# Order of the first chunks in a hybrid pool and RG-LRU layer: block 9 weights ahead of token tiles, root diagonals one chunk early, chunk 1 normalised ahead of chunk 0's evacuation

## The chip, the core and the metric

One core of one Trainium2 chip runs the whole layer in one launch. The metric is the device time of that launch in microseconds (us), as a median over several runs. The engines are named as in the profile: PE (matmul) and PEld (its weight load), DVE (VectorE), ACT (ScalarE), POOL (GpSimd), SP (SyncE, which issues all DMAs here).

## The reference, cut to what matters

A layer of one prompt (2048 tokens) and eight short samples (8 tokens each), so 2112 tokens of width 1024:

```python
xn = rms_norm(x, norm_pre)                  # one factor 1/rms per token, one gain per channel
z  = xn @ w_in                              # 1024 -> 4096: pool values, pool gate, lru input, lru gate
y_pool = pool_mixer(z[0:1024])              # windows of 2/4/8/16 tokens, then a 256x256 map per group
y_lru  = rg_lru(causal_conv(z[2048:3072]))  # gates, then a scan over the tokens
mixed  = concat(y_pool * silu(z[1024:2048]), y_lru * silu(z[3072:4096]))
out    = x + rms_norm(mixed @ w_out, norm_post)
```

## The kernel before, in words

Tokens lie along the free dimension in five chunks of 426 (the last has 408); `xn[c]` holds a chunk's normalised inputs in 8 slices `k` of 128 channels. Every product is made from a high and a low part of both operands (`hi = round(x)`, `lo = x - hi`), so a slice costs three matmuls of 426 columns, and one block of 128 output channels of one chunk (`z_k` over `k`, lines 287 to 293) costs 24. Blocks 0 and 1 are the values ("v"), blocks 8 and 9 the gates ("g") of pool group 0.

The 1/rms factors are per token and so lie along columns. They come from a second copy of x with tokens on partitions, in 17 tiles of 128 tokens (`load_tok`, 512 KB each, three slots of three tiles). ACT squares and sums a tile (`tok_square`, line 224); `tok_rsqrt` (lines 226 to 234) makes the factors of a range of tiles with four small DVE and two small ACT instructions; `r_rows(c)` (lines 236 to 246) makes a chunk's row of factors on all partitions: ACT scales pieces of the identity by the factors (line 243, tile `dg`), and PE multiplies an all-ones matrix by each piece (line 245, tile `r` in PSUM). `normalise(c)` (lines 248 to 275) then scales the raw chunk on DVE (line 261), ACT rounds it to the high part (line 269), and DVE or POOL subtracts for the low part (line 278). It can take squares of later tiles along on ACT. Two tiles of `x` are therefore needed before a chunk can start: its transposed copy (`xt`) and the token tiles that it covers.

Chunk 0 is different: its slices are multiplied by the channel gain only (`x_g`, `x_hi`, `x_lo`, lines 592 to 600), the matmuls start at once, and the factors are applied when the four results are read out of PSUM (`pool_evac`, line 323, and line 705, with `r0`, a copy in SBUF of the row of chunk 0). Later, at chunk 2, `normalise(0, r0)` scales chunk 0 for the other blocks.

Everything from line 607 to line 789 is in a `manual_schedule`: each engine runs its instructions in the order in which the lines issue them, and each engine's queue waits in that order. SP's queue holds the loads, in the order of the lines 608 to 630: weights and chunk 0 interleaved, then block 8, token tiles 0 to 3, half of chunk 1, tiles 4 and 5, the other half, tile 6, block 9 (`w9r`), the first pool map, chunk 2. PE's queue: v of chunk 0, block 8 (line 684), block 9 (line 692) with the rows of chunks 0 and 1 after its third slice (`R01_AT`), then v of chunk 1, `r_rows(2)`, gate block 8 of chunk 1, the pool map of chunk 0 (`pool_mm`, tile `y`), gate block 9, and then chunks 2, 3 and 4 (lines 714 to 789), where `r_rows(c + 1)` stands after the last slice of the first value block.

PSUM has two rings of four banks: `z_psum` and `s_psum`.

Of the kernel before, what the change touches and what calls it, by code (L numbers as in the profile page):

```python
# [16 lines left out]
P = 128  # L17
# [44 lines left out]
def hymba_kernel(  # L62
# [19 lines left out]
    nc = tc.nc  # L82
# [152 lines left out]

    def r_rows(c):
        lo, hi = XR[c]
        dg = tp_tile(f"dg{c}")
        R = s_psum(f"r{c}")[:, :hi - lo]
        for i in range(lo // P, (hi - 1) // P + 1):  # L240
            n = min(P, T_ALL - i * P)
            a, b = max(lo, i * P), min(hi, i * P + n)
            nc.scalar.activation(out=dg[:n, a - lo:b - lo], in_=ident[:n, a - i * P:b - i * P], func=AF.Copy,
                                 scale=tok[:n, 2, i:i + 1])
            nc.tensor.matmul(R[:, a - lo:b - lo], lhsT=ones[:n, :], rhs=dg[:n, a - lo:b - lo], start=True, stop=True)
        return R
# [360 lines left out]
    with tc.manual_schedule():  # L607
        stage_w(0, 0, 1)
        load_x(0, 0, 1)
        nc.sync.dma_start(out=parT, in_=par)  # L610
        load_x(0, 1, 2)
        stage_w(1, 0, 1)
        load_x(0, 2, 4)
# [5 lines left out]
        for i in range(4):  # L619
            load_tok(i, slots[i // 3])  # L620
        load_x(1, 0, 4)
        for i in range(4, 6):
            load_tok(i, slots[1])
        load_x(1, 4, 8)
        load_tok(6, slots[2])
        for h in range(2):
            nc.sync.dma_start(out=w9r[h], in_=w_in[9, :, 512 * h:512 * (h + 1)])
        pw0r = raw_tile("pw0r")
        nc.sync.dma_start(out=pw0r, in_=pool_w[0])
        load_x(2, 0, 8)  # L630
        w_hi(0, 0, A)
        w_lo(0, 0, V)
        x_g(0)
        x_hi(0)
        x_g(1)
        x_hi(1)
        x_lo(0, V)
# [25 lines left out]
        w_hi(8, 0, A)  # L663
        w_lo(8, 0, G)
        for i in range(3):
            tok_square(i)
        w_hi(8, 1, A)
        w_lo(8, 1, G)
# [5 lines left out]
        lag = 3  # L674
# [10 lines left out]
        for h in range(2):  # L685
            w_hi(9, h, A)
            w_lo(9, h, G)
        for k in range(KT):
            if k == R01_AT:
                R0, r1 = r_rows(0), r_rows(1)  # L690
                A.copy(out=r0, in_=R0)
            z_k(Z0[3], wt[9], 0, k)
        Es, sgs0 = [], []
# [3 lines left out]
        normalise(1, r1, [V], {3: (7,), 5: (8,), 7: (9,)})  # L697
# [16 lines left out]
        for c in range(1, NCH):  # L714
            n = c + 1 if c < LAST else None
            W = CHUNKS[c][1] - CHUNKS[c][0]
            Z = [z_psum(f"v{j}_{c}")[:, :W] for j in range(2)]
# [16 lines left out]
            if c == 1:  # L734
# [3 lines left out]
                tok_rsqrt(7, 10)  # L738
# [21 lines left out]
            if c == 1:  # L760
# [3 lines left out]
                tok_rsqrt(10, 17)  # L764
                silus()
# [708 lines left out]
```

## Time and profile before

| what | value |
|---|---|
| median of 3 runs | 1203.39 us (1202.67 to 1204.98) |
| profiled execution, its own time | 1200.54 us |
| span of that execution (first to last instruction) | 1198.7 us |
| PE busy | 1169.1 us, 98% of the span |
| DVE, ACT, POOL busy | 829.1, 552.3, 356.5 us |
| mean granted TensorE clock | 0.991 of full speed |

The profiled execution is 2.85 us under the median; 1.84 us of it lie outside the span. All positions below are us from the span's start. A bracket at the end of a timeline row is the idle time of the engine before it and what ended that.

### The profile page before, as it was taken

To read this page: it belongs to the slowest core of one execution; us is meant where nothing else is said; L and a number is where in the kernel's file an instruction comes from. 1 tells how busy PE (TensorE), PEld (TensorE's weight loads), DVE (VectorE), ACT (ScalarE), POOL (GpSimd) and SP (SyncE) were. 2 spreads that over 40 slices of the span, in tenths; PEclk is the share of its full clock that TensorE was granted. 3 is DMA by queue.
4 is the path that set the end of the run, shared out by engine and by line. 5 is a ranking of instruction groups with operands and counts; after the bars stand their busy time and mean duration, and the time that the engine had idled before them with its cause. 6 is when DMAs were issued, how large, how long until landed. Compare 5 with 4: busy or idle time off the path is not lost.

```text
span 1198.7 us, 16264 instructions
## 1 busy us (share of the span) xinstructions
PE 1169.1 (98%) x5794; PEld 1079.4 (90%) x5794; DVE 829.1 (69%) x1201; ACT 552.3 (46%) x1015; POOL 356.5 (30%) x486
## 2 busy tenths in 40 slices
PE   6898999999999999999999999999999999999997
PEld 5798999999999999999999999999978878888886
DVE  4666453435445546888888888889877668887787
ACT  5663221221231125767767676776755243335232
POOL 3224430531251232344333433344310002221332
PEclk9799999999999999999999999999999999999999
DMA  9612353533541110111111111113479767767553
GB/s 338 238 42 73 110 190 117 175 101 118 162 129 52 44 42 33 53 49 44 44 41 45 35 50 49 44 40 105 138 202 296 219 185 205 217 198 232 150 170 129
DMA packets 127905, 146.94 MB, mean 123 GB/s; under 512 B 12432, under 2 KB 87440, under 8 KB 127824
## 3 DMA queue, kind: packets, MB, share of 16 engines
q1 hardware_dynamic: 127824, 145.91, 39.1%
q8 instruction: 45, 0.74, 0.3%
q14 instruction: 36, 0.29, 0.1%
HBM read 106.37 MB, written 39.24 MB: 121 GB/s over the span
## 4 chain that ended last, share of the span: by engine, by line
PE 77%; DVE 8%; DMA 6%; ACT 3%; issue 2%; POOL 1%; SPq 0%; DVEq 0%; ACTq 0%; POOLq 0%
PE p L964 6%; PE p L963 6%; PE p L962 6%; PE u L291 5%; PE u L293 5%; PE u L292 5%; PE lg L291 5%; PE lg L292 4%; PE lg L293 4%; PE v L291 4%; PE v L293 4%; PE v L292 4%; PE g L291 4%; PE g L293 4%; PE g L292 4%; DMA a<-mixed 3%
## 5 line engine op out<-in xcount | busy, mean ns | idle before, releaser
L493 DVE SCALAR_TENSOR_TENSOR xs<-u,parT,xs 128x426 f32<-128x426 f32 (+1 forms) x120 | 109.4, 911 | 46.1 <-ACT xs L489 30.5
L291 PE MATMUL v<-xh,w 128*128 128x426 f32 (+2 forms) x320 | 116.7, 365 | 7.9 <-ACT xh L596 7.5
L291 PE MATMUL g<-xh,w 128*128 128x426 f32 (+1 forms) x320 | 115.4, 361 | 3.1 <-ACT w L584 3.1
L292 PE MATMUL v<-xl,w 128*128 128x426 f32 (+2 forms) x320 | 116.0, 363 | 1.3 <-DVE xl L600 0.7
L955 POOL TENSOR_TENSOR xr<-ac,xr 128x512 f32<-128x512 f32 x28 | 47.6, 1717 | 228.6 <-DVE ac L1093 130.7
L293 PE MATMUL g<-xh,w 128*128 128x426 f32 (+1 forms) x320 | 114.8, 359 | 0.3 <-POOL w L587 0.3
L292 PE MATMUL g<-xl,w 128*128 128x426 f32 (+1 forms) x320 | 114.5, 358 | 0.0
L291 PE MATMUL lg<-xh,w 128*128 128x426 f32 (+1 forms) x320 | 113.7, 355 | 0.0
L293 PE MATMUL v<-xh,w 128*128 128x426 f32 (+2 forms) x320 | 113.7, 360 | 0.0
L291 PE MATMUL u<-xh,w 128*128 128x426 f32 (+1 forms) x320 | 113.7, 355 | 0.0
L292 PE MATMUL lg<-xl,w 128*128 128x426 f32 (+1 forms) x320 | 113.4, 354 | 0.0
L293 PE MATMUL lg<-xh,w 128*128 128x426 f32 (+1 forms) x320 | 113.2, 354 | 0.0
L293 PE MATMUL u<-xh,w 128*128 128x426 f32 (+1 forms) x320 | 113.1, 353 | 0.0
L292 PE MATMUL u<-xl,w 128*128 128x426 f32 (+1 forms) x320 | 113.0, 353 | 0.0
L1255 DVE RECIPROCAL rv<-rv 128x426 f32<-128x426 f32 (+1 forms) x40 | 112.4, 2811 | 0.0
L962 PE MATMUL p<-ws,s 128*128 128x512 f32 (+1 forms) x264 | 102.4, 388 | 0.0
L963 PE MATMUL p<-ws,s 128*128 128x512 f32 (+1 forms) x264 | 102.0, 386 | 0.2 <-DVE ws L109 0.2
L964 PE MATMUL p<-ws,s 128*128 128x512 f32 (+1 forms) x264 | 102.1, 387 | 0.1
L962 PE MATMUL p<-ws,a 128*128 128x512 f32 x192 | 75.7, 394 | 1.0 <-ACT ws L106 1.0
L964 PE MATMUL p<-ws,a 128*128 128x512 f32 x192 | 75.8, 395 | 0.8 <-DVE a L109 0.8
L963 PE MATMUL p<-ws,a 128*128 128x512 f32 x192 | 75.7, 394 | 0.4 <-DVE ws L109 0.4
L354 DVE TENSOR_TENSOR s<-e 128x440 f32<-128x440 f32 (+3 forms) x40 | 29.2, 730 | 66.9 <-ACT e L325 48.2
(225 smaller groups left out, 2810.8 us busy)
## 6 DMA issues: line engine op xcount, KB each, us to landing
a<-mixed SPq DMA_DIRECT2D x112, 256.0 KB, 4.2
wr<-in_w_in SPq DMA_DIRECT2D x56, 256.0 KB, 3.1
tok<-in_x SPq DMA_DIRECT2D x16, 512.0 KB, 11.1
wo<-in_w_out SPq DMA_DIRECT2D x32, 256.0 KB, 3.6
wtd<-wo SPq DMA_DIRECT2D x32, 256.0 KB, 2.4
w<-wtd SPq DMA_DIRECT2D x32, 256.0 KB, 3.7
xr<-in_x SPq DMA_DIRECT2D x32, 256.0 KB, 3.7
out<-xr SPq DMA_DIRECT2D x30, 256.0 KB, 2.6
```

What stands on the lines that cost most here:

```text
L291: nc.tensor.matmul(out, lhsT=wh, rhs=xh, start=(k == 0), stop=False)
L292: nc.tensor.matmul(out, lhsT=wh, rhs=xl, start=False, stop=False)
L293: nc.tensor.matmul(out, lhsT=wl, rhs=xh, start=False, stop=(k == KT - 1))
L354: nc.vector.tensor_tensor(out=dst[:, first:L], in0=src[:, first:L], in1=src[:, first - sh:L - sh], op=ALU.add)
L493: nc.vector.scalar_tensor_tensor(out=xs, in0=E[:, k:k + n], scalar=col(C_CW + 8 * k, b), in1=xs, op0=ALU.mult, op1=ALU.add)
L955: (eng or nc.vector).tensor_tensor(out=out, in0=a, in1=b, op=op)
L962: nc.tensor.matmul(out, lhsT=ah, rhs=wh, start=start and k == 0, stop=False)
L963: nc.tensor.matmul(out, lhsT=ah, rhs=wl, start=False, stop=False)
L964: nc.tensor.matmul(out, lhsT=al, rhs=wh, start=False, stop=stop and k == KT - 1)
L1255: nc.vector.reciprocal(out=v, in_=v)
```

## The change

It changes the order in which instructions are issued between the launch and chunk 3, and four places where a piece stands:

- SP's loads: `par` and the first slice of chunk 0 come first; slices 2 and 3 come ahead of block 1's first half; three token tiles, then block 9's weights, then tiles 3 to 6 with chunk 1's first half among them, and chunk 1's second half behind tile 6.
- DVE and ACT take the first slice of chunk 0 ahead of block 0's weights. Block 8's and block 9's weights are both split before token tile 3 is squared. The second value block starts four slices behind the first (`lag`), not three.
- `r_rows` is cut in two: `r_diag(c)` has the ACT instructions, `r_rows(c)` the matmuls. The diagonals of chunks 1 and 0 stand ahead of block 9; those of chunks 2, 3 and 4 one chunk earlier than their matmuls.
- The row of chunk 1 is made ahead of the row of chunk 0, and `normalise(1)` stands ahead of the evacuation of chunk 0's values. The values of chunk 1 lie in the `s` ring of PSUM, no longer in the `z` ring. `tok_rsqrt(7, 10)` moves from behind the matmuls of chunk 1 to behind that evacuation.

```diff
+    diags = {}
+
+    def r_parts(c):
+        lo, hi = XR[c]
+        for i in range(lo // P, (hi - 1) // P + 1):
+            n = min(P, T_ALL - i * P)
+            yield i, n, max(lo, i * P), min(hi, i * P + n)
+
+    def r_diag(c):
+        lo = XR[c][0]
+        dg = diags[c] = tp_tile(f"dg{c}")
+        for i, n, a, b in r_parts(c):
+            nc.scalar.activation(out=dg[:n, a - lo:b - lo], in_=ident[:n, a - i * P:b - i * P], func=AF.Copy,
+                                 scale=tok[:n, 2, i:i + 1])
     def r_rows(c):
...
+        for i, n, a, b in r_parts(c):
+            nc.tensor.matmul(R[:, a - lo:b - lo], lhsT=ones[:n, :], rhs=diags[c][:n, a - lo:b - lo],
+                             start=True, stop=True)
...
+        nc.sync.dma_start(out=parT, in_=par)
+        load_x(0, 0, 1)
         stage_w(0, 0, 1)
-        load_x(0, 0, 1)
-        nc.sync.dma_start(out=parT, in_=par)
         load_x(0, 1, 2)
+        load_x(0, 2, 4)
         stage_w(1, 0, 1)
-        load_x(0, 2, 4)
...
-        for i in range(4):
-            load_tok(i, slots[i // 3])
-        load_x(1, 0, 4)
-        for i in range(4, 6):
-            load_tok(i, slots[1])
-        load_x(1, 4, 8)
-        load_tok(6, slots[2])
+        for i in range(3):
+            load_tok(i, slots[0])
         for h in range(2):
             nc.sync.dma_start(out=w9r[h], in_=w_in[9, :, 512 * h:512 * (h + 1)])
+        load_tok(3, slots[1])
+        load_x(1, 0, 4)
+        for i in range(4, 7):
+            load_tok(i, slots[i // 3])
+        load_x(1, 4, 8)
...
-        w_hi(0, 0, A)
-        w_lo(0, 0, V)
         x_g(0)
         x_hi(0)
+        w_hi(0, 0, A)
+        x_lo(0, V)
+        w_lo(0, 0, V)
         x_g(1)
         x_hi(1)
-        x_lo(0, V)
...
-        w_hi(8, 0, A)
-        w_lo(8, 0, G)
+        for h in range(2):
+            w_hi(8, h, A)
+            w_lo(8, h, G)
         for i in range(3):
             tok_square(i)
-        w_hi(8, 1, A)
-        w_lo(8, 1, G)
+        for h in range(2):
+            w_hi(9, h, A)
+            w_lo(9, h, G)
...
-        lag = 3
+        lag = 4
...
-        for h in range(2):
-            w_hi(9, h, A)
-            w_lo(9, h, G)
+        r_diag(1)
+        r_diag(0)
         for k in range(KT):
             if k == R01_AT:
-                R0, r1 = r_rows(0), r_rows(1)
+                r1, R0 = r_rows(1), r_rows(0)
                 A.copy(out=r0, in_=R0)
             z_k(Z0[3], wt[9], 0, k)
+        normalise(1, r1, [V], {3: (7,), 5: (8,), 7: (9,)})
...
-        normalise(1, r1, [V], {3: (7,), 5: (8,), 7: (9,)})
+        tok_rsqrt(7, 10)
+        r_diag(2)
...
-            Z = [z_psum(f"v{j}_{c}")[:, :W] for j in range(2)]
+            Z = [(s_psum if c == 1 else z_psum)(f"v{j}_{c}")[:, :W] for j in range(2)]
...
-                tok_rsqrt(7, 10)
...
                 tok_rsqrt(10, 17)
+                r_diag(3)
                 silus()
...
             if c == 2:
+                r_diag(4)
                 normalise(0, r0, [G])
```

Three places in the engines' order follow. In them `tok_108` to `tok_110` are the token slots, `dg` the diagonals, `r_111` the copy `r0`, `pw` the pool map, `dh` the high part of a windowed chunk, `xh` and `xr` the high part and raw slices of a chunk.

ACT from the squares of the token tiles 3 to 6 to the copies of chunk 1, before:

```order
L224 ACTIVATE tok_109,tok<-tok_109 128x1024 x3
L224 ACTIVATE tok_110,tok<-tok_110 128x1024
L230 ACTIVATE tok<-tok 128x7
L231 ACTIVATE tok<-tok 128x7
L584 CAST w_0_104<-w9r_96 128x512
L584 CAST w_1_105<-w9r_97 128x512
L243 ACTIVATE dg_295<-ident,tok 128x128 x3
L243 ACTIVATE dg_295<-ident,tok 128x42
L243 ACTIVATE dg_305<-ident,tok 128x86
L243 ACTIVATE dg_305<-ident,tok 128x128 x2
L243 ACTIVATE dg_305<-ident,tok 128x84
L691 COPY r_111<-r_296 128x426
```

and now:

```order
L595 CAST w_0_104<-w9r_96 128x512
L595 CAST w_1_105<-w9r_97 128x512
L224 ACTIVATE tok_109,tok<-tok_109 128x1024 x3
L224 ACTIVATE tok_110,tok<-tok_110 128x1024
L230 ACTIVATE tok<-tok 128x7
L231 ACTIVATE tok<-tok 128x7
L248 ACTIVATE dg_286<-ident,tok 128x86
L248 ACTIVATE dg_286<-ident,tok 128x128 x2
L248 ACTIVATE dg_286<-ident,tok 128x84
L248 ACTIVATE dg_291<-ident,tok 128x128 x3
L248 ACTIVATE dg_291<-ident,tok 128x42
L703 COPY r_111<-r_310 128x426
```

Block 9's two casts went ahead of the squares of tiles 3 to 6, and the diagonals of chunk 1 (86 + 128 + 128 + 84 columns) ahead of those of chunk 0.

ACT from the square of tile 9 to the copies of chunk 1's values (`e_1`), before:

```order
L224 ACTIVATE tok_109,tok<-tok_109 128x1024 x3
L106 CAST pw_369<-pw0r 128x512
L106 CAST dh_0_383<-d_0_378 128x426
L106 CAST dh_0_394<-d_0_389 128x426
L230 ACTIVATE tok<-tok 128x3
L231 ACTIVATE tok<-tok 128x3
L243 ACTIVATE dg_454<-ident,tok 128x44
L243 ACTIVATE dg_454<-ident,tok 128x128 x2
L243 ACTIVATE dg_454<-ident,tok 128x126
L325 COPY e_1_464<-v_1_398 128x426
```

and now:

```order
L224 ACTIVATE tok_109,tok<-tok_109 128x1024
L230 ACTIVATE tok<-tok 128x3
L231 ACTIVATE tok<-tok 128x3
L248 ACTIVATE dg_370<-ident,tok 128x44
L248 ACTIVATE dg_370<-ident,tok 128x128 x2
L248 ACTIVATE dg_370<-ident,tok 128x126
L224 ACTIVATE tok_109,tok<-tok_109 128x1024 x2
L106 CAST pw_380<-pw0r 128x512
L106 CAST dh_0_394<-d_0_389 128x426
L106 CAST dh_0_405<-d_0_400 128x426
L336 COPY e_1_464<-v_1_409 128x426
```

The factors and diagonals of chunk 2 stand directly behind the square of tile 9, ahead of two more squares, of the pool map and of chunk 0's windows.

ACT in chunk 2, around `normalise(0)` (the casts `xh_106`), before:

```order
L106 CAST dh_2_737<-d_2_735 128x426
L269 CAST xh_106<-xr_119 128x852 x4
L243 ACTIVATE dg_813<-ident,tok 128x104
L243 ACTIVATE dg_813<-ident,tok 128x128 x2
L243 ACTIVATE dg_813<-ident,tok 64x64
```

and now:

```order
L106 CAST dh_2_737<-d_2_735 128x426
L248 ACTIVATE dg_771<-ident,tok 128x104
L248 ACTIVATE dg_771<-ident,tok 128x128 x2
L248 ACTIVATE dg_771<-ident,tok 64x64
L280 CAST xh_106<-xr_119 128x852 x4
```

The diagonals of chunk 4 went ahead of the four casts of chunk 0.

## Rows read from the trace of the kernel before

**Rows 1.** The page's first part: busy time and share of the span of each engine, and its instructions.

```profile
PE 1169.1 (98%) x5794; PEld 1079.4 (90%) x5794; DVE 829.1 (69%) x1201; ACT 552.3 (46%) x1015; POOL 356.5 (30%) x486
```

**Rows 2.** Who waited for whom, PE's own waits of the whole span, the three largest: who, for whom, us in total, times, longest.

```profile
PE v L291 <- ACT xh L596: 7.5, 2, 6.1
PE r L245 <- ACT dg L243: 7.4, 3, 3.3
PE g L291 <- ACT w L584: 3.1, 1, 3.1
```

**Rows 3.** Timeline of PE: start, duration, line, operation, tiles, shape, count, and idle time before it. Durations overlap; the pace is read from start to start.

```profile
30.32 0.72 PE L291 MATMUL g<-xh,w 128*128 128x426 f32 x1 [3.15 <-ACT w L584]
...
40.18 0.35 PE L291 MATMUL v<-xh,w 128*128 128x426 f32 x1
43.43 0.46 PE L292 MATMUL v<-xl,w 128*128 128x426 f32 x1 [0.57 <-DVE xl L278]
...
53.78 0.65 PE L245 MATMUL r<-dg,ones 128*128 128x44 f32 x2 [3.29 <-ACT dg L243]
56.52 0.70 PE L291 MATMUL g<-xh,w 128*128 128x426 f32 x1
57.02 0.56 PE L292 MATMUL g<-xl,w 128*128 128x426 f32 x1
59.86 0.56 PE L291 MATMUL g<-xh,w 128*128 128x426 f32 x1
...
65.50 0.36 PE L291 MATMUL g<-xh,w 128*128 128x426 f32 x1
70.15 0.36 PE L291 MATMUL v<-xh,w 128*128 128x426 f32 x1
...
100.41 1.56 PE L245 MATMUL r<-dg,ones 128*128 128x104 f32 x8 [3.32 <-ACT dg L243]
```

**Rows 4.** Stretches of the span: length, busy time and instructions of PE, PEld, DVE, ACT, POOL, granted TensorE clock, DMA share, GB/s.

```profile
29.90:36.73 6.83, 6.14 (x21) 5.40 (x22) 0.45 (x4) 3.60 (x11) 2.55 (x3) 0.50 1.04 391
36.73:53.79 17.06, 13.20 (x70) 12.14 (x69) 15.57 (x27) 10.92 (x21) 3.84 (x6) 1.00 0.68 264
53.79:60.62 6.83, 6.04 (x20) 5.63 (x21) 4.59 (x9) 4.25 (x9) 1.20 (x5) 0.50 0.00 0
...
101.58:105.00 3.42, 3.42 (x11) 3.12 (x12) 1.22 (x2) 0.83 (x3) 1.77 (x4) 0.50 0.00 0
```

**Rows 5.** Timeline of DVE, columns as in the timeline of PE.

```profile
8.01 0.72 DVE L584 CAST w<-wst 128x512 fp32r<-128x512 f32 x1 [0.66 <-DMA wst<-in_w_in]
9.45 1.22 DVE L593 TENSOR_SCALAR x0g<-xr,parT 128x426 f32<-128x426 f32 x2 [0.72 <-DMA xr<-in_xt]
...
30.19 0.17 DVE L234 SCALAR_TENSOR_TENSOR tok<-tok 128x7 f32<-128x7 f32 x1
...
37.70 1.22 DVE L261 SCALAR_TENSOR_TENSOR xr<-xr,parT,r 128x426 f32<-128x426 f32 x2
...
46.45 1.10 DVE L705 TENSOR_TENSOR sg<-g,r 128x426 f32<-128x426 f32 x2
...
83.11 2.36 DVE L261 SCALAR_TENSOR_TENSOR xr<-xr,parT,r 128x426 f32<-128x426 f32 x4
93.21 2.44 DVE L261 SCALAR_TENSOR_TENSOR xr<-xr,parT,r 128x426 f32<-128x426 f32 x1
```

**Rows 6.** DMA issues of the whole span by line: tiles, queue, count, KB each, median us from issue to landing. The first is the two halves of chunk 1, the second block 9's weights.

```profile
xr<-in_xt SPq DMA_DIRECT2D x2, 852.0 KB, 11.4
...
w9r<-in_w_in SPq DMA_DIRECT2D x2, 256.0 KB, 11.1
```

**Rows 7.** Timeline of ACT, columns as in the timeline of PE. The first is the square of token tile 6, the fourth that of tile 9.

```profile
27.92 1.06 ACT L224 ACTIVATE tok<-tok 128x1024 f32<-128x1024 f32 x1 [2.37 <-DMA tok<-in_x]
...
30.69 2.30 ACT L243 ACTIVATE dg<-ident,tok 128x128 f32<-128x128 f32 x8
36.13 0.52 ACT L691 COPY r<-r 128x426 f32<-128x426 f32 x1 [3.14 <-PE r L245]
...
45.36 1.05 ACT L224 ACTIVATE tok<-tok 128x1024 f32<-128x1024 f32 x1
...
48.49 0.60 ACT L106 CAST pw<-pw0r 128x512 fp32r<-128x512 f32 x1
...
54.77 0.98 ACT L243 ACTIVATE dg<-ident,tok 128x128 f32<-128x128 f32 x3 [1.04 <-DVE tok L234]
...
99.98 1.20 ACT L243 ACTIVATE dg<-ident,tok 128x104 f32<-128x104 f32 x4
```

**Rows 8.** The one load of a token tile issued at 27.98 us (tile 9): duration in ns, start in us; and its time to landing.

```profile
L220 SPq DMA_DIRECT2D tok<-in_x x1: 5507/5507/5507, 28.0 to 28.0; - x1
...
DMA to landing us min/median/max: 15.3/15.3/15.3
```

**Rows 9.** Timeline of POOL, same columns.

```profile
49.17 1.45 POOL L109 TENSOR_TENSOR pw<-pw0r,pw 128x512 fp32r<-128x512 f32 x1 [11.12 <-ACT pw L106]
...
53.24 1.08 POOL L109 TENSOR_TENSOR dl<-d,dh 128x426 fp32r<-128x426 f32 x1 [1.22 <-ACT dh L106]
...
83.00 2.09 POOL L278 TENSOR_TENSOR xl<-xr,xh 128x852 fp32r<-128x852 f32 x1 [1.43 <-ACT xh L269]
```

More of the change, by code (lines that the diff above doesn't have):

```diff
@@ L234, in tok_rsqrt @@
         V.scalar_tensor_tensor(out=r, in0=u, scalar=1.5, in1=r, op0=ALU.add, op1=ALU.mult)
+    diags = {}
[10 more added lines that the diff above has]
+                                 scale=tok[:n, 2, i:i + 1])
     def r_rows(c):
         lo, hi = XR[c]
-        dg = tp_tile(f"dg{c}")
         R = s_psum(f"r{c}")[:, :hi - lo]
[L240 to L245, printed above, removed]
+        for i, n, a, b in r_parts(c):
+            nc.tensor.matmul(R[:, a - lo:b - lo], lhsT=ones[:n, :], rhs=diags[c][:n, a - lo:b - lo],
+                             start=True, stop=True)
         return R
```

## The prediction

> **What bounds the kernel now.** I read four views, in this order. The page's first part says that PE is busy for 98% of the span [rows 1]: the time is PE's work plus PE's waits. The list of PE's own waits [rows 2] has three large entries: 7.5 us for chunk 0's first high parts, 7.4 us for the rows of factors (tile `r`, behind ACT's diagonals), 3.1 us for block 9's weights. The timeline of PE [rows 3] shows where they lie: 3.15 us before 30.32, 3.29 us before 53.78, 3.32 us before 100.41, and a small one of 0.57 us before 43.43. The stretches [rows 4] show what each large one brings with it: the granted clock is 0.50, the lower level (1.2 GHz), for 6.83 us from 29.90, for 6.83 us from 53.79 and for 3.42 us from 101.58; in the 17.06 us around the 0.57 us gap it is 1.00 (2.4 GHz). The pace follows from PE's starts [rows 3]: 24 matmuls from 65.50 to 70.15, so 0.194 us each at the upper level; 8 from 57.02 to 59.86, so 0.355 at the lower. A microsecond at the lower level thus loses 0.45 us. Two places carry the sum: the start of chunk 2's values, at 70.15, and the row of chunk 4 at 100.41. What lies between and behind is the same PE work in both kernels, and its inputs follow PE's own results, so I carry a gain there to the end.
>
> **Part 1, the first slices: later by 0.75 to 1.1 us, absorbed.** With `par` and the first slice loaded first, the first matmul comes some 0.6 us earlier, but the third slice decides. DVE still casts block 1's weights ahead of it, and the two loads swap: that cast started at 8.01 when its weights landed, the slices at 9.45 when theirs did [rows 5]. Now the weights come second, at 9.45, the cast takes 0.72, and the third slice follows at 10.2 instead of 9.45. The longer `lag` leaves one slice of the second block more (3 x 0.194 = 0.6 us) behind the last low part. Block 8 ended at 30.32 - 3.15 = 27.2; I expect 28.2. The ends are 27.2 (DVE makes it up) and 30.7 (the clock also rises one stretch later, 2.5 us more). None of them moves the next point by more than 1.5 us.
>
> **Part 2, block 9 and the rows of chunks 0 and 1: 5.3 us.** Block 9's weights now lie ahead of token tile 3, so PE goes on at once: 9 matmuls, and it meets the rows at about 29.9. What is late next is token tile 6, whose landing ACT awaited at 27.92 [rows 7]. In SP's queue the second half of chunk 1 (852 KB) went behind it and block 9 (2 x 256 KB) ahead of it [rows 6]: 340 KB less, at 391 GB/s [rows 4] 0.9 us, so its square starts at 27.0. From that square to finished factors were 30.19 + 0.17 - 27.92 = 2.44 us [rows 5, 7], now 29.5; block 9's casts no longer stand between, and eight diagonals take 2.30 [rows 7], to 31.8. PE ends the rows at 32.0, does its remaining 15 matmuls (2.9 us) and starts chunk 1's values at 34.9 instead of 40.18 [rows 3]. With part 1 at its late end it would be 36.5. `normalise(1)` has chunk 1's row at 31.0, since that row is made first; ACT's copy of `r0` (0.52 [rows 7]) stands ahead of its first high part, at 32.6. DVE started 2.5 us ahead of PE before (37.70 against 40.18 [rows 3, 5]) and now nearly 4, so the 0.57 us gap goes.
>
> **Part 3, the row of chunk 2: 9.3 us in all by here.** 48 matmuls of chunk 1 take 9.3 us, to 44.3. DVE needs 8.75 us for `normalise(1)` (37.70 to 46.45 [rows 5]), and the evacuation of chunk 0 that now follows costs 1.1 us more, like the pair at 46.45: DVE is free at about 42. The new wait is tile 9. It landed at 28.0 + 15.3 = 43.3 [rows 8]; the same bytes stand ahead of it in both queues, and the DMA engines are full in that stretch [rows 4], so it lands at 43.3 again. Square 1.15, factors 1.28 (as in part 2), four diagonals 1.20 [rows 7]: 46.95, and PE ends the row at 47.2 instead of 56.52. Part 1 at its late end is absorbed here (45.8 is still before the first diagonal at 46.1). PE idles about 2 us. What a gap of that size does to the clock the trace doesn't show: 0.57 left it at 1.00, 3.15 to 3.32 brought 0.50 for 3.42 to 6.83 us [rows 3, 4]. The ends are 0 and 6.83 x 0.45 = 3.1 us; I take 3.42 us at the lower level, 1.55 us, since 2 us is nearer to the long gaps and the shortest spell belongs to work that then ran on unbroken.
>
> **Part 4, chunk 0's pool map: 9.85 us in all by here.** ACT's queue behind the diagonals holds two squares (1.05 each), the pool map's cast (0.60 [rows 7]) and two casts of windows; DVE has the first window ready by 48.3 (gates 1.10 [rows 5] and about 1.4 from 45.8 on). POOL takes the map's low part at 49.8 (1.45) and two windows' low parts (1.08 to 1.45 each [rows 9]): 53.7. PE reaches the map at 47.2 + 24 x 0.194 = 51.9 with the clock up, and waits 1.2 us in two pieces; or at 53.4 with 3.42 us at the lower level, and waits for nothing. So the clock and the map cost much the same time once, not twice: the map (12 matmuls) ends at 55.3 or 55.7, gate block 9 4.65 us later, and chunk 2 starts at 60.0 or 60.35. I take 60.3 against 70.15.
>
> **Part 5, the row of chunk 3: nothing, with 1.7 us to spare.** `normalise(2)` starts at 49.7 and runs as long as `normalise(1)`, to 59.4 with the first low part held by POOL; two squares, factors and diagonals end at 63.2, PE comes at 65.0. The cover is thinner than before, because POOL works beside it now. Four instructions of that kind took 2.36 us beside a POOL subtraction of 2.09 [rows 5, 9], no longer than without; at 93.21 a single one took 2.44 [rows 5]. The first reads its factors in PSUM, the second `r0` in SBUF, and chunk 2's factors are in PSUM. The Trainium skill (SBUF — State Buffer, section "SBUF: two separate sides") says that VectorE and GpSimd share one pair of ports, which a VectorE operation with two SBUF inputs or a GpSimd operation holds to its end. By that rule only the low parts can be held and the sum stays 15.3 us; by 93.21 alone, the scalings too would be held for POOL's three operations, chunk 3's row would be 1.5 us late, and the sum would be 13.8. The two durations agree with the rule.
>
> **Part 6, the row of chunk 4: 5.5 us.** ACT made these diagonals (99.98, 1.20 us [rows 7]) behind the casts of `normalise(0)`, which waited for DVE's held scalings (93.21 [rows 5]). Now they stand ahead of them, some 8 us before PE comes. The wait of 3.32 goes, the 3.42 us at the lower level (1.55) and the slow row itself (1.56 us of matmuls [rows 3], half at the upper level, about 0.7). The casts come 1.2 us later; no product needs them before the other groups.
>
> **Costs nothing.** Chunk 1's values in the `s` ring: the next row takes the bank of chunk 1's row (read to about 40), the maps take `r0`'s (copied at 32.6) and the first value bank (read by ACT at 51.4, needed after 52).
>
> **Sum.** 9.85 + 5.5 = 15.3 us: 1200.54 becomes 1185.2 for the profiled execution. The median of the runs is 2.85 us above that execution, so I forecast 1203.39 - 15.3 = **1188.1 us**.
>
> **Rivals.** (a) *The middle is longer*: the clock stays at the lower level for 6.83 us behind the gap, as from 53.79, or chunk 3's row is late because the scalings are held as at 93.21. For it: two of three spells were that long. Against: the long ones had a second short wait inside. Block 8 of chunk 1 would then end at 54.9, chunk 2 start at 61.8, gain 13.8: 1189.6; with both, up to 1191. (b) *The change doesn't do what it says at chunk 4*: the diagonals move, but PE's wait at 100.41 was put down to ACT's last instruction and has another cause. For it: only the bracket of one row names ACT. Against: that chain is seen link by link. Gain 9.85: 1193.5. (c) *Tile 9 is earlier*, since the loads end in a tighter stream; a microsecond earlier moves chunk 2 by as much until the map holds it: 1186.5. (d) *Slower*: the new short gaps (third slice, first rows, row of chunk 2) keep the clock at the lower level from the start until chunk 2. Its price: some 190 matmuls x 0.161 and 2 us of rows, less 3.5 us of gaps that fill up, 29 us, so 14 us slower: 1217. It decides once about half of these run at the lower level. For it: the clock came back only 6.83 us after two of the gaps. Against: it stayed at 1.00 over the 0.57 us gap [rows 4]. (e) *No change*: some later stage, bound by another engine, takes the gain back: 1203; against it stands PE's 98%.
>
> **How the numbers follow.** Forecast 0.66 (1186.5 to 1189.5 by itself, with the ends of parts 3 and 4 and the spread of the runs), (a) 0.17, (b) 0.07, (c) 0.06, (d) 0.02, (e) 0.02. The range runs from (c), less the 0.7 us by which runs fall below their median, to (b): 1185.5 to 1193.5. A measurement of this kernel tells some 0.2% (2.4 us) from no change: faster 0.96, same 0.02, slower 0.02.
>
> **What would show it.** PE's wait for block 9 gone; chunk 1's values from about 34.9; one wait of about 2 us before the row of chunk 2, ended by ACT, with tile 9 landing near 43.3; chunk 2 from about 60.3; no wait at the rows of chunks 3 and 4. Wrong would be: a wait of over 1 us at chunk 0's pool map together with the lower clock, a wait at the row of chunk 4, or a gain by chunk 2 that is smaller at the end.

## The result and the profile after

The changed kernel takes **1188.92 us** (median of 4 runs, 1186.45 to 1190.4) against 1203.03 us for the kernel before (1201.93 to 1204.98): ratio 0.9884, 95% interval 0.9864 to 0.9904. The forecast was 1188.1. Its profiled execution took 1190.4 us, with a span of 1188.4 and a mean granted clock of 0.997 (0.991 before).

In its profile the line numbers are shifted: matmuls are L302 to L304 (L291 to L293 before), the row's matmuls L255, its diagonals L248, the scaling of `normalise` L272, its high and low parts L280 and L289. First the page's engine line, as in [rows 1]: PE is busy 2.0 us less, and the span is 10.3 us shorter, so most of what went was PE's waiting (a matmul at the lower clock counts as busy).

```profile
PE 1167.1 (98%) x5794; PEld 1076.0 (91%) x5794; DVE 828.8 (70%) x1201; ACT 552.4 (46%) x1015; POOL 356.9 (30%) x486
```

PE's own waits of the whole span, as in [rows 2]:

```profile
PE v L302 <- ACT w L595: 6.0, 1, 6.0
PE r L255 <- ACT dg L248: 1.6, 2, 1.2
...
PE f L316 <- ACT wth L106: 1.2, 1, 1.2
...
PE v L302 <- ACT xh L607: 0.6, 2, 0.4
```

The wait for block 9's weights (3.1) is gone, that for the rows went from 7.4 to 1.6. The 6.0 at the head is the launch's first wait, under another name than before. The timeline of PE, as in [rows 3], with the starts that the forecast named:

```profile
11.18 0.72 PE L303 MATMUL v<-xl,w 128*128 128x426 f32 x1 [0.58 <-DVE xl L611]
...
23.65 0.36 PE L302 MATMUL g<-xh,w 128*128 128x426 f32 x1
...
30.06 1.87 PE L255 MATMUL r<-dg,ones 128*128 128x86 f32 x16
...
34.77 0.35 PE L302 MATMUL v<-xh,w 128*128 128x426 f32 x1
...
45.60 0.42 PE L255 MATMUL r<-dg,ones 128*128 128x44 f32 x2 [1.19 <-ACT dg L248]
46.40 1.38 PE L255 MATMUL r<-dg,ones 128*128 128x128 f32 x6 [0.38 <-ACT dg L248]
47.43 0.70 PE L302 MATMUL g<-xh,w 128*128 128x426 f32 x1
...
53.51 0.36 PE L316 MATMUL y<-dh,pw 128*128 128x426 f32 x1
...
60.53 0.36 PE L302 MATMUL v<-xh,w 128*128 128x426 f32 x1
...
87.32 1.19 PE L255 MATMUL r<-dg,ones 128*128 128x104 f32 x8
...
104.88 0.35 PE L302 MATMUL v<-xh,w 128*128 128x408 f32 x1
```

The reader is to see: no bracket at 30.06 (rows of chunks 0 and 1), at 53.51 (pool map) and at 87.32 (row of chunk 4, 3.32 us before); one gap in two pieces, 1.19 and 0.38, at the row of chunk 2. Chunk 1 starts at 34.77 (40.18 before, 34.9 forecast), chunk 2 at 60.53 (70.15; 60.3 forecast), chunk 4 at 104.88 (119.74, so 14.86 earlier; 15.3 forecast). The stretches around the gap, columns as in [rows 4]:

```profile
20.00:46.91 26.91, 25.34 (x138) 23.96 (x136) 12.12 (x26) 17.95 (x41) 3.50 (x7) 1.00 1.04 396
46.91:50.32 3.41, 3.41 (x12) 3.25 (x12) 2.93 (x10) 3.41 (x9) 0.73 (x1) 0.50 0.15 60
50.32:60.00 9.68, 9.68 (x51) 9.36 (x51) 8.87 (x12) 9.41 (x16) 4.09 (x7) 1.00 0.30 84
```

One spell at the lower level (1.2 GHz), of 3.41 us, is left where there were three of 6.83, 6.83 and 3.42 us (both executions have one more in their last 8 us). Then the timeline of ACT, as in [rows 7]: the square of tile 6, the diagonals of chunks 1 and 0, the square of tile 9, three diagonals of chunk 2.

```profile
26.15 1.06 ACT L224 ACTIVATE tok<-tok 128x1024 f32<-128x1024 f32 x1
...
28.69 2.31 ACT L248 ACTIVATE dg<-ident,tok 128x86 f32<-128x86 f32 x8 [0.70 <-DVE tok L234]
...
43.49 1.06 ACT L224 ACTIVATE tok<-tok 128x1024 f32<-128x1024 f32 x1 [3.27 <-DMA tok<-in_x]
...
45.94 0.98 ACT L248 ACTIVATE dg<-ident,tok 128x128 f32<-128x128 f32 x3 [0.40 <-DVE tok L234]
```

Tile 9 is what the row of chunk 2 now waits for: ACT idles 3.27 us for its landing, and from 43.49 the chain square, factors, diagonals runs straight to PE's 45.60 and 46.40. Last the timeline of DVE, as in [rows 5]: block 1's cast and the third slice; `normalise(2)`'s first four scalings and its first low part.

```profile
8.41 0.48 DVE L595 CAST w<-wst 128x512 fp32r<-128x512 f32 x1 [1.40 <-DMA wst<-in_w_in]
8.82 1.80 DVE L604 TENSOR_SCALAR x0g<-xr,parT 128x426 f32<-128x426 f32 x2
...
50.10 2.37 DVE L272 SCALAR_TENSOR_TENSOR xr<-xr,parT,r 128x426 f32<-128x426 f32 x4 [0.34 <-issue]
52.38 1.57 DVE L289 TENSOR_TENSOR xl<-xr,xh 128x852 fp32r<-128x852 f32 x1
```

### The profile page after: what moved, and what is told of

It reads as the page before. It is cut to its first block, busy times and chain, and to the rows that moved or that the text cites. A ratio compares the mean times of both kernels' runs of the same rounds, so it can differ in the third digit from the quotient of the medians.

```text
span 1188.4 us, 16263 instructions
## 1 busy us (share of the span) xinstructions
PE 1167.1 (98%) x5794; PEld 1076.0 (91%) x5794; DVE 828.8 (70%) x1201; ACT 552.4 (46%) x1015; POOL 356.9 (30%) x486
## 4 chain that ended last, share of the span: by engine, by line
PE 84%; DVE 5%; DMA 5%; ACT 3%; issue 2%; POOL 1%; SPq 0%; DVEq 0%; ACTq 0%; POOLq 0%
PE p L979 7%; PE p L978 7%; PE p L977 7%; PE v L302 5%; PE v L304 5%; PE v L303 5%; PE u L302 5%; PE u L304 5%; PE u L303 5%; PE g L302 5%; PE lg L302 5%; PE lg L304 5%; PE lg L303 5%; PE g L303 5%; PE g L304 5%
## 5 line engine op out<-in xcount | busy, mean ns | idle before, releaser
L302 PE MATMUL v<-xh,w 128*128 128x426 f32 (+2 forms) x320 | 116.9, 365 | 7.1 <-ACT w L595 6.0
L302 PE MATMUL g<-xh,w 128*128 128x426 f32 (+1 forms) x320 | 114.6, 358 | 0.0
L304 PE MATMUL v<-xh,w 128*128 128x426 f32 (+2 forms) x320 | 114.1, 362 | 0.4 <-DVE w L109 0.4
L304 PE MATMUL g<-xh,w 128*128 128x426 f32 (+1 forms) x320 | 113.9, 356 | 0.2 <-POOL w L109 0.2
L302 PE MATMUL u<-xh,w 128*128 128x426 f32 (+1 forms) x320 | 113.7, 355 | 0.0
L302 PE MATMUL lg<-xh,w 128*128 128x426 f32 (+1 forms) x320 | 113.7, 355 | 0.0
L304 PE MATMUL lg<-xh,w 128*128 128x426 f32 (+1 forms) x320 | 113.5, 355 | 0.0
L304 PE MATMUL u<-xh,w 128*128 128x426 f32 (+1 forms) x320 | 113.4, 354 | 0.0
## 6 DMA issues: line engine op xcount, KB each, us to landing
tok<-in_x SPq DMA_DIRECT2D x16, 512.0 KB, 10.2
```

The source lines that it names most:

```text
L302: nc.tensor.matmul(out, lhsT=wh, rhs=xh, start=(k == 0), stop=False)
L304: nc.tensor.matmul(out, lhsT=wl, rhs=xh, start=False, stop=(k == KT - 1))
```

## The experiments

Twelve runs followed, each against the kernel before on the same chip. The theory was the prediction's chain: the diagonals made early (chunks 2 and 4), with tile 9's landing as the new bound of the row of chunk 2. The rivals were that the gain comes from the load order, from the clock, or from DVE's order. The table puts them together; "chunk 4" is the start of chunk 4's values in the profiled execution (119.74 before), and the gain of the median is against the runs of before in the same batch. Batches ran on different chips, so kernels of different batches are compared by their gains.

| run | what differs | chunk 2 | chunk 4, earlier by | median (range) | gain of median | ratio, 95% |
|---|---|---|---|---|---|---|
| again | the changed kernel | 59.16 | 16.23 | 1188.07 (1185.77–1190.43) | 14.1 | 0.9863–0.9902 |
| e1_diag4 | before + `r_diag(4)` early | 69.73 | 5.68 | 1198.28 (1194.7–1198.68) | 3.8 | 0.9945–0.9974 |
| e2_nodiag4 | changed, `r_diag(4)` late | 60.48 | 9.66 | 1194.68 (1192.27–1195.6) | 7.4 | 0.9918–0.995 |
| e11_nodiag2 | changed, `r_diag(2)` late | 65.93 | 9.46 | 1194.61 (1194.09–1196.2) | 7.0 | 0.9927–0.9962 |
| e4_first | changed, first slices as before | 60.97 | 14.44 | 1188.12 (1186.46–1191.06) | 14.0 | 0.9858–0.9899 |
| e5_loads | changed, loads as before | 59.48 | 15.91 | 1187.47 (1185.63–1190.86) | 16.1 | 0.9852–0.9888 |
| e6_late | changed, `normalise(1)` late | 58.92 | 16.47 | 1188.29 (1185.44–1188.8) | 15.0 | 0.9867–0.9901 |
| e3_tile9 | changed, tile 9 early | 58.04 | 17.35 | 1185.64 (1183.76–1186.34) | 18.0 | 0.9831–0.9865 |
| e9_late_tile9 | e3 + `normalise(1)` late | 58.60 | 16.79 | 1186.52 (1184.79–1187.43) | 16.7 | 0.9848–0.9885 |
| e7_map | e3 + pool map early | 57.94 | 17.09 | 1186.79 (1184.53–1187.49) | 16.8 | 0.9841–0.9877 |
| e8_best | e7 + earlier loads | 57.54 | 17.82 | 1184.1 (1183.29–1188.72) | 19.5 | 0.983–0.9869 |
| e10_copies | e8, squares 10, 11 later | 57.11 | 17.36 | 1186.64 (1184.29–1188.37) | 16.6 | 0.9848–0.9888 |

Two columns carry the first result: what a kernel has gained by chunk 4 is its gain at the end to between 2.5 us less and 1.7 us more. What the first chunks do decides the time; the rest is spread and a slow drift (see below).

**again**: the changed kernel once more.

> The changed kernel once more, for its spread and for what happens behind chunk 3. By PE's starts it was 14.9 us ahead of the kernel before at chunk 4 (104.88 against 119.74 us), but its profiled execution ended only 10.3 us ahead; 2.4 us of the rest were lost in two waits near 140 and 243 us. Theory: these waits are spread from run to run (loads that land a little earlier or later), so chunk 4 starts at 104.9 again, within 0.3 us, the waits differ, and the median gain lies at 13 to 15.5 us. Rival: they are the price of the change (the stage behind is bound by its loads and gives 2 to 4 us back each time): the same two waits with 1 us or more each, and a gain of 10 to 12 us.

The median came out within 1 us, but chunk 4 started at 103.51, outside what I expected: the clock did not fall behind the gap. PE's two waits and the stretch behind them in this execution:

```profile
45.29 0.42 PE L255 MATMUL r<-dg,ones 128*128 128x44 f32 x2 [0.83 <-ACT dg L248]
46.09 1.07 PE L255 MATMUL r<-dg,ones 128*128 128x128 f32 x6 [0.38 <-ACT dg L248]
```

```profile
46.91:50.32 3.41, 3.41 (x20) 3.30 (x20) 2.92 (x9) 3.41 (x8) 1.03 (x1) 1.00 0.27 109
```

Against the same stretch of the first execution: 20 matmuls instead of 12 in 3.41 us, granted 1.00 instead of 0.50. Gaps of 0.83 and 0.38 left the clock up, 1.19 and 0.38 did not. Chunk 2 is 1.37 us earlier; 0.31 us of that lie ahead of the clock, since the row started at 45.29 and not at 45.60 (tile 9 landed earlier), and 1.06 us come behind it. The two waits near 140 and 243 us that the rival asked for came as 0.41 and 0.38 us, not as 1 us each: they are not a fixed price of the change.

**e1_diag4 and e2_nodiag4**: the diagonals of chunk 4 alone, on the kernel before and taken out of the changed one.

```diff
 # e1_diag4: before, with r_rows cut in two and each r_diag(c) directly ahead of its r_rows(c), except
             if c == 2:
+                r_diag(4)
                 normalise(0, r0, [G])
 # e2_nodiag4: the changed kernel
-                r_diag(4)
                 normalise(0, r0, [G])
+                r_diag(4)
```

> The kernel before with one edit: the diagonals of chunk 4 stand ahead of the normalising of chunk 0. Theory: PE's wait of 3.32 us before 100.41, the fall of the clock behind it (1.55 us) and the row's own matmuls at the lower level (0.7 us) all go, nothing else: chunk 2 starts at 70.15 as before, chunk 4 at 114.2 instead of 119.7, and the time falls by 5.5 us to about 1197.5. Rival: the row is late for another reason than ACT's order (its factors, or a bank): no change, 1203.

> The changed kernel with that one edit undone: the diagonals of chunk 4 stand behind the casts of chunk 0 again. Theory: chunk 3 starts at 82.7 as in the changed kernel, the row of chunk 4 waits some 3 us for ACT and the clock falls behind it: 4.8 to 5.5 us are lost, about 1194. Rival: with everything 9.6 us earlier the normalising of chunk 0 is ready in time, the edit was worth little in this place and the front gave more than I summed: 1189 to 1190.

In e1 the row of chunk 4 runs from 96.51 without a wait and chunk 4 is 5.68 us earlier. In e2 the old picture comes back inside the changed kernel, at PE's row and in the stretch behind it:

```profile
90.78 1.61 PE L255 MATMUL r<-dg,ones 128*128 128x104 f32 x7 [3.35 <-ACT dg L248]
```

```profile
91.58:94.99 3.41, 3.41 (x11) 2.93 (x11) 1.22 (x2) 1.20 (x3) 2.13 (x4) 0.50 0.00 0
```

From the start of chunk 2 to that of chunk 4 it is 49.59 us in the kernel before and 49.60 in e2, 44.33 in e1 and 44.35 in the changed kernel: wait, slow row and slow stretch together make 5.25 us, in either surrounding. The forecast had 5.5. The medians move by 3.8 (e1) and by about 6 (e2 against the changed kernel). The rival that this edit does nothing is out.

**e11_nodiag2**: the factors and diagonals of chunk 2 back in the loop.

```diff
-        tok_rsqrt(7, 10)
-        r_diag(2)
...
                         z_k(Z[j], wt[j], c, k)
+                tok_rsqrt(7, 10)
+                r_diag(2)
                 r = r_rows(n)
```

> The changed kernel with one part undone: the factors and diagonals of chunk 2 (tok_rsqrt(7, 10), r_diag(2)) go back into the loop, on ACT and DVE behind the squares of tiles 10 and 11, the map's cast and the windows of chunk 0. Theory (this move, and not the loads of block 9, carries most of the gain before chunk 2): the values of chunk 1 still end near 44.3, but the diagonals come only at 49 to 51.2, PE waits 4.5 to 6 us for them, the row ends at 51.0 to 52.2 instead of 47.4, the clock falls to its lower level for 3.4 to 6.8 us, chunk 2 starts at 64.5 to 67 instead of 60.5, chunk 4 at 109 to 111.5 instead of 104.9, and the median is 5 to 6.5 us above the changed kernel's 1188: 1193 to 1195. Rival (tile 9 and the squares set the row either way): chunk 2 at most 2 us later and a median of 1190.

Chunk 2 started at 65.93 (60.53), the median rose to 1194.61: as the theory had it, with 6.2 us of waits at the row (4.5 to 6 expected). PE, then DVE, then POOL, then the stretch of the lower clock:

```profile
48.65 0.42 PE L255 MATMUL r<-dg,ones 128*128 128x44 f32 x2 [4.23 <-ACT dg L248]
51.06 1.65 PE L255 MATMUL r<-dg,ones 128*128 128x128 f32 x6 [2.00 <-ACT dg L248]
```

```profile
48.60 0.93 DVE L233 SCALAR_TENSOR_TENSOR tok<-tok 128x3 f32<-128x3 f32 x1
49.57 1.01 DVE L234 SCALAR_TENSOR_TENSOR tok<-tok 128x3 f32<-128x3 f32 x1
```

```profile
47.21 1.26 POOL L109 TENSOR_TENSOR pw<-pw0r,pw 128x512 fp32r<-128x512 f32 x1 [5.44 <-ACT pw L106]
48.44 2.12 POOL L109 TENSOR_TENSOR dl<-d,dh 128x426 fp32r<-128x426 f32 x2
```

```profile
49.50:56.33 6.83, 5.27 (x17) 5.03 (x18) 4.62 (x8) 4.12 (x9) 1.73 (x6) 0.50 0.00 0
```

Tile 9 had landed at 42.9, so here it is the queue that waits, not the load. Two DVE instructions on three columns take 0.93 and 1.01 us instead of 0.16 while POOL subtracts, and that is most of the second wait, 2.00 us where the changed kernel has 0.38. Where a small DVE step stands in the order counts twice, for its place and for what POOL does at that time.

**e4_first, e5_loads, e6_late**: three parts undone, one at a time.

```diff
 # e4_first: loads and slice order of the start as before
-        nc.sync.dma_start(out=parT, in_=par)
-        load_x(0, 0, 1)
         stage_w(0, 0, 1)
+        load_x(0, 0, 1)
+        nc.sync.dma_start(out=parT, in_=par)
...
-        lag = 4
+        lag = 3
 # e5_loads: block 9 (loads and casts), tiles 3 to 6 and chunk 1 in the order of before
-        for i in range(3):
-            load_tok(i, slots[0])
-        for h in range(2):
-            nc.sync.dma_start(out=w9r[h], in_=w_in[9, :, 512 * h:512 * (h + 1)])
...
         load_tok(6, slots[2])
+        for h in range(2):
+            nc.sync.dma_start(out=w9r[h], in_=w_in[9, :, 512 * h:512 * (h + 1)])
 # e6_late
-        normalise(1, r1, [V], {3: (7,), 5: (8,), 7: (9,)})
         Es, sgs0 = [], []
...
+        normalise(1, r1, [V], {3: (7,), 5: (8,), 7: (9,)})
         tok_rsqrt(7, 10)
```

> The changed kernel with the first slices as before: load order of the first six loads, block 0's weights ahead of slice 0, lag 3. Theory: the value blocks of chunk 0 end 1.3 us earlier (22.35 instead of 23.65 us), PE then waits that much longer for the rows of chunks 0 and 1, which token tile 6 holds, and chunk 1 starts at 34.8 as before: no change, within 0.5 us of the changed kernel. Rival: tile 6 is not what holds PE there, and the earlier end passes to the end: 1.3 us faster. Second rival: the new order of the first slices carries a part of the gain: slower by 1 us or more.

> The changed kernel with the loads of block 9, token tiles 0 to 6 and chunk 1 in the order of before, and block 9's casts behind the factors again. Theory: PE's wait for block 9 comes back (2 us or more before 30.3). If the clock stays up, chunk 1 starts at 36.4 instead of 34.8 and tile 9 absorbs it: no change. If it falls as in the kernel before, chunk 1 starts at about 40, the row of chunk 2 ends 3 us later, and 3 us are lost. So 0 to 3 us slower. Rival: the front's gain is made by these loads alone, which then costs the 5 us by which chunk 1 starts earlier in the changed kernel: 5 us slower or more.

> The changed kernel with one part undone: normalise(1) goes back behind the evacuation of chunk 0's values (2 x 0.55 us on DVE). Theory (tile 9 sets the row of chunk 2, not DVE): PE waits some 0.5 to 1.5 us at the first slices of chunk 1, the values of chunk 1 start up to 1 us later (about 35 to 36) and end by 46, tile 9 still lands near 43.5, so the row of chunk 2 still ends near 47.0 and chunk 2 starts at 59.2 to 60.5, within 0.5 us of the changed kernel; median 1187.5 to 1189.5. Rival (the order of DVE is worth its microsecond): chunk 2's start and the median 1 to 1.5 us later, 1190.

None of the three moved the time beyond its spread. In e4 chunk 0's values ended 1.3 us earlier (22.33) and chunk 1 still started at 35.03, because PE now waited for the diagonals behind tile 6, as the theory had it:

```profile
29.86 2.35 PE L255 MATMUL r<-dg,ones 128*128 128x86 f32 x16 [0.96 <-ACT dg L248]
```

The clock fell behind the row of chunk 2 as in the first execution of the changed kernel.

In e6 DVE's lost microsecond showed as three waits of PE, 1.0 us in all, in the values of chunk 1, which ended at 46.09 instead of 44.25; but the diagonals behind tile 9 ended only at 46.4, so the row ended at 46.90, as in the second execution (46.91), and nothing was lost. e5 is the one to look at. PE at block 9 and at the row of chunk 2:

```profile
29.88 0.46 PE L302 MATMUL g<-xh,w 128*128 128x426 f32 x1 [1.36 <-ACT w L595]
...
31.23 0.46 PE L304 MATMUL g<-xh,w 128*128 128x426 f32 x1 [0.70 <-POOL w L598]
...
46.88 1.05 PE L255 MATMUL r<-dg,ones 128*128 128x44 f32 x8
```

PE waits 2.06 us for the old, late weights, and chunk 1 starts 2.6 us late (37.40; I had expected 36.4). The row of chunk 2 then needs no wait at all, since the diagonals behind tile 9 had ended at 46.3, and ends at 47.69; in the changed kernel it ended at 47.43 and 46.91. So here PE's own lateness sets the row, and it takes the place of the wait for tile 9. Of the 2.6 us at chunk 1, 0.3 are left at chunk 2 against the second execution (59.48 and 59.16, both with the clock up). By itself the load order showed no more than that, with tile 9 landing at 42.4 to 43.9 in these kernels.

**e3_tile9 and e9_late_tile9**: tile 9 earlier, by one 1704 KB load put behind three of 512 KB.

```diff
 # e3_tile9
         for i in range(7, 9):
             load_tok(i, slots[2])
-        load_x(3, 0, KT)
...
         for i in range(9, 12):
             load_tok(i, slots[1])
+        load_x(3, 0, KT)
 # e9_late_tile9: e3_tile9 with the edit of e6_late
```

> The changed kernel with one load moved: chunk 3's inputs (1704 KB) behind token tiles 9 to 11 in SP's queue instead of ahead of them. Theory: tile 9's landing (43.5 us in the changed kernel) is what the row of chunk 2 waits for; it falls by 4.4 us to about 38, and the row then waits for the factors behind the evacuation of chunk 0 alone: it ends at about 45 instead of 46.9 to 47.4. Chunk 0's pool map loses its cover and waits about 1.3 us, so chunk 2 starts at 57.4 to 58 instead of 59.2 (clock up) or 60.5 (clock down): 1.5 to 3 us faster. Rival: the row waits for DVE (normalising and evacuation stand ahead of its factors), tile 9 is hidden behind that: no change.

> The changed kernel with the load of chunk 3 behind tiles 9 to 11 (as in e3_tile9) and normalise(1) back behind the evacuation of chunk 0's values. Theory: with tile 9 early the cover of the undone part is gone, so the values of chunk 1 end 0.5 to 1.5 us later than in e3_tile9 (45.4 there) and the row of chunk 2 with them; chunk 2 starts at 58.5 to 59.5 against 58.04 in e3_tile9, and the median is 0.5 to 1.5 us above that kernel's 1185.6: 1186 to 1187, still below the changed kernel's 1188. Rival (DVE is off the path either way): chunk 2 at 58.0 again and a median of 1185.6.

ACT's square of tile 9, then PE's row of chunk 2, of e3:

```profile
40.49 1.05 ACT L224 ACTIVATE tok<-tok 128x1024 f32<-128x1024 f32 x1
```

```profile
45.45 1.05 PE L255 MATMUL r<-dg,ones 128*128 128x44 f32 x8
```

The tile landed at 38.33, neither row has a bracket, the clock stayed at 1.00, chunk 2 started at 58.04. The wait of 1.3 us at the pool map that I had expected did not come. The gain of the median is 3.9 us above the changed kernel's two. In e9 PE waits for DVE's low parts again (0.18, 0.22, 0.65) and the row ends 0.56 us later than in e3, although its chunk 1 started 1.2 us earlier (34.78; e3's start had lost time at the third slice). With tile 9 out of the way the order of DVE has a price, 0.6 to 1.7 us at chunk 2, which the gains of the medians (1.3 apart, ranges that overlap) can't prove.

**e7_map, e8_best, e10_copies**: what is late next.

```diff
 # e7_map: e3_tile9, and
+        pw0 = split_small(pw0r, 512, "pw0")
         tok_rsqrt(7, 10)
         r_diag(2)
-        for i in range(10, 12):
-            tok_square(i)
...
-        pw0 = split_small(pw0r, 512, "pw0")
...
             ds0.append(pool_window(j, 0, 0, Es[j]))
+        for i in range(10, 12):
+            tok_square(i)
 # e8_best: e7_map, the start as in e4_first, and
-        load_tok(3, slots[1])
-        load_x(1, 0, 4)
-        for i in range(4, 7):
+        for i in range(3, 7):
             load_tok(i, slots[i // 3])
+        load_x(1, 0, 4)
         load_x(1, 4, 8)
 # e10_copies: e8_best, the squares of tiles 10 and 11 behind the two evac(j) of chunk 1
```

> As the kernel before this one but one (chunk 3's inputs behind tile 11), and the pool map's cast ahead of chunk 2's factors, with the squares of tiles 10 and 11 behind the casts of chunk 0's windows. Theory: the map's wait of 1.3 us goes too: chunk 2 at 56.8 to 57.2, 0.6 to 1 us more than with the load alone, 2.5 to 3.7 us faster than the changed kernel. Rival: ACT is not the limit there, the windows on DVE are: the same as with the load alone.

> The version with the most behind it: as the one just above, with the first slices in the order of before and token tiles 3 to 6 ahead of both halves of chunk 1. Theory: tile 6 lands at 23.8 instead of 26.1, so PE's own work (first slices, block 8) decides the rows of chunks 0 and 1: chunk 1 at 32.9 instead of 34.8, the row of chunk 2 ends at 43.4, chunk 2 starts at 55: 4 to 5.5 us faster than the changed kernel, about 1183.5. Rival: the halves of chunk 1 now land too late for its normalising (26 and 28.4 us), chunk 1 waits for low parts, and it gives less than the version above.

> The kernel e8_best with one edit: the squares of tiles 10 and 11 on ACT go behind its copies of chunk 1's values (e, two of 1.1 us), which freed the bank that a value block's map waited for (0.50 us at 51.63, in two places). Theory (that bank was the last wait before chunk 2): the map of chunk 0 runs without a wait of over 0.2 us, chunk 2 starts at 56.6 to 57.1 instead of 57.54, chunk 4 at 101.0 to 101.5 instead of 101.92, and the median is 0.5 to 1 us below e8_best: 1183 to 1183.8, less than the spread of the runs can prove. Rival (windows): the map waits for POOL's low part of the windows instead and chunk 2 stays at 57.5.

e7 and e8 missed at chunk 2 (57.94 for 56.8 to 57.2, 57.54 for 55), and e7's median is not below e3's. The rows of e8 say why, ACT first and then PE in the pool map:

```profile
43.79 0.99 ACT L248 ACTIVATE dg<-ident,tok 128x128 f32<-128x128 f32 x3 [1.17 <-DVE tok L234]
...
50.05 1.05 ACT L224 ACTIVATE tok<-tok 128x1024 f32<-128x1024 f32 x1
...
51.09 0.91 ACT L336 COPY e<-v 128x426 f32<-128x426 f32 x2
```

```profile
51.63 0.46 PE L316 MATMUL y<-dh,pw 128*128 128x426 f32 x1 [0.50 <-ACT e L336]
```

The map's second result takes the PSUM bank of chunk 1's first values, and ACT copies those out behind the squares that e7 had moved. That is the smaller part of e8's miss. The larger stands ahead of it: PE waits 0.62 us for a low part of chunk 1 at 39.04, as the rival had it, and 0.35 us for diagonals, and the row of chunk 2 ends at 45.08, not at 43.4. Those diagonals wait 1.17 us for their factors (43.79), because e7's edit brings POOL's subtraction of the map beside the small DVE steps, and one of them takes 0.93 us, as in e11:

```profile
42.44 0.93 DVE L232 TENSOR_TENSOR tok<-tok 128x3 f32<-128x3 f32 x1 [0.51 <-ACT tok L231]
```

```profile
42.06 1.28 POOL L109 TENSOR_TENSOR pw<-pw0r,pw 128x512 fp32r<-128x512 f32 x1
```

In e10 the copies start at 49.32 and the map has no wait; chunk 2 starts at 57.11, 0.43 earlier, as forecast. But chunk 4 starts at 102.38, 0.46 later than in e8 (101.0 to 101.5 expected), because the moved squares hold up what stands behind them on ACT, and the row of chunk 3 now waits:

```profile
62.67 1.22 PE L255 MATMUL r<-dg,ones 128*128 128x128 f32 x8 [0.47 <-ACT dg L248]
```

So the edit moved a wait more than it removed one. Its median is 2.5 us above e8's. Its profiled execution waited 1.14 us at 241.28 and the clock fell for 3.42 us there, which e8's did not; what its other runs met isn't shown. e8 has the lowest median, 1184.1 us, but e3, e7, e8, e9 and e10 overlap in their intervals, so their order is not settled.

## Why the prediction was right

**Part 1, absorbed, by another path.** The chunk's values ended 1.3 us later (0.75 to 1.1 forecast), but not by the third slice: the weights landed 1 us earlier than I took from the swap, and the slice started at 8.82, not 10.2. PE's idle time in these blocks was smaller than before (1.48 us against 2.11, the 0.58 at 11.18 among it). What came late was the clock, by PE's pace: its matmuls went from 0.355 to 0.194 us apart at 19.5 instead of 16.3, which by the forecast's 0.45 is 1.4 us. I had put that case at the far end, with 30.7 for the end of block 8; it came at about 28.3 (28.2 forecast). e4 shows that it costs nothing by chunk 2.

**Part 2, right to 0.15 us, with two bounds where I had one.** Tile 6 landed at 26.13 (forecast 27.0), the diagonals ended at 31.0, and PE came to the rows at 30.06 from its own work. I had chunk 1 wait on tile 6; in the first execution it waited for nothing. In the second it did, as forecast: 0.22 us, and a row of 2.35 us instead of 1.87; in e4 0.96 us. In the changed kernel PE's own work and tile 6 come within a microsecond of each other.

**Part 3, right.** Tile 9 landed at 43.47 (43.3), PE idled 1.57 us (about 2), the row ended at 47.43 (47.2). e3 shows the cause: 5 us earlier landing, no gap. e11 shows the price of the move: 5.4 us at chunk 2 (6.8 against the second execution). The clock term (1.55 us, from ends of 0 and 3.1) held in the first execution (3.41 us at the lower level), not in the second. It has no single value.

**Part 4, right at 60.3 for the case that came first, wrong for the other.** With 3.41 us at the lower clock PE reached the map at 53.51 (53.4) without a wait, and chunk 2 started at 60.53 (60.35). I had the map hold chunk 2 to 60.0 if the clock stayed up, so that clock and map cost the same once. POOL was through by 53.0, not 53.7, and with the clock up PE waited 0.2 us at the map, not 1.2: chunk 2 at 59.16. The clock costs 1.06 us there, not 0.35.

**Part 5, right.** PE came to the row of chunk 3 2.4 us after its diagonals (forecast 1.7). The four scalings at 50.10 took 2.37 us with POOL busy from 50.87 on, the low part behind them 1.57 instead of 1.03 to 1.04. In e11 two operations with both inputs in SBUF took 0.93 and 1.01 us instead of 0.16. The Trainium skill (SBUF — State Buffer, section "SBUF: two separate sides") says that a VectorE operation with two SBUF inputs and a GpSimd operation that reads SBUF lock out each other for the whole instruction. These durations agree with it, and the scalings, with their factors in PSUM, were not held.

**Part 6, right.** 5.5 forecast; 5.25 in the changed kernel, e1 and e2 alike.

**The sum.** 15.3 forecast; 14.86 and 16.23 at chunk 4; 14.1 in both medians. The step that was too simple is "I carry a gain there to the end". Lined up with the kernel before, matmul by matmul, the first profiled execution lost 4.5 us of its lead later: 1.1 by 158 (waits at block weights), 1.6 by 256 (a wait of 1.25 us for `wth` at 244), the rest in slow drift and behind 880. The second lost 3.6 us: 0.9 by 145, 1.4 in drift, the rest around 887 (a wait of 1.78 us with a spell of 3.41 us at the lower clock). These waits are for casts of newly loaded data; their place changes from execution to execution, and the kernel before has its own. Why a given one falls there wasn't settled.

The drift is not chance. Between the same two matmuls of PE, some 560 us apart, the changed kernel takes 1.0 us longer than e4, which has the first slices as before. The changed kernel first, then e4:

```profile
308.08 0.36 PE L304 MATMUL g<-xh,w 128*128 128x426 f32 x1
...
869.22 0.40 PE L978 MATMUL p<-ws,a 128*128 128x512 f32 x1
```

```profile
309.21 0.36 PE L304 MATMUL g<-xh,w 128*128 128x426 f32 x1
...
869.39 0.40 PE L978 MATMUL p<-ws,a 128*128 128x512 f32 x1
```

It is 561.1 to 561.2 us in all nine executions with the new first slices, and 560.1 to 560.2 in all five with the old ones (the kernel before, e1, e4, e8, e10). So part 1, absorbed by chunk 2, costs about 1 us behind chunk 4, through a cause that no run shows; too little for e4's median to prove. It is also a part of e8's lead over e3, 0.5 us at chunk 4 and 2.7 us at the end of the profiled executions.

That the median met the forecast to 0.8 us is in part luck: for the profiled execution the forecast was 1185.2, and the two took 1190.4 and 1188.0. The step from there to the median took over 2.85 us from the kernel before; in the changed kernel the first profiled execution lay 1.5 us above its median. (The lower end of the range, by its own sum, is 1185.8.)

Of the rivals, (a) did not come: the spell was of 3.41 us or none, and the scalings ran on. (b), (d) and (e) are out by e1, e2 and the result. (c) did not happen by itself; e3 made it happen, with 5.1 us instead of one, and came to 1185.6, near the 1186.5 that I had priced. Not tried alone: the `s` ring for chunk 1's values, the swap of the rows of chunks 0 and 1, and the diagonals of chunk 3. And the 4.2 us that e11 still has at chunk 2 (65.93 against 70.15) were not taken apart: each of e4, e5 and e6 undoes one part while the others cover for it.

## What to carry to other kernels

Look at the instruction that releases the long wait, and ask what stands ahead of it in its own engine's queue: two small steps of ACT (the diagonals of chunks 2 and 4) that had their inputs early but stood behind other work cost 5.4 and 5.25 of the 14.9 us when each was put back, each with its wait and the clock's spell behind it. Then find what is late next (here one token tile behind a 1704 KB load) before pricing the other edits: the load order, the first slices and DVE's order showed no gain while that tile was the last to come, and the first slices cost 1 us later on. And a gain that is read at one place of one execution needs several runs behind it: it reached the end within 2.5 us, no closer.

## What the runs showed of the hardware

- What a short gap does to the clock can't be read from one execution. At the row of chunk 2 the granted clock fell to 0.50 after 0.97 + 0.38 us (e2), 1.19 + 0.38 (first execution) and 1.36 + 0.38 (e4), and stayed at 1.00 after 0.83 + 0.38 (second execution); at block 9 it stayed at 1.00 after 1.36 + 0.70 (e5, 1 us of work between). After 3.35 us (e2) it fell for 3.41 us, after 4.23 + 2.00 (e11) for 6.83.
- One 1704 KB load moved behind three token tiles brought the landing of tile 9 from 43.47 to 38.33 us (5.1 us), and PE showed no new wait for it.
- A three-column DVE operation with both inputs in SBUF took 0.93 to 1.01 us instead of 0.16 beside POOL's subtraction (e11, e8).
